# The first query chunk of two head blocks handled together in the self-attention of a hybrid decoder step

## The chip, the cores and the metric

The kernel runs on one core of one Trainium2 chip. The metric is device time in microseconds (us) for one launch, which computes the whole step. Three runs of the kernel before gave 1402.44, 1402.56 and 1403.07 us; the median is 1402.56 us. The profiled execution is one more run, of 1402.98 us, and its trace spans 1401.2 us from the first to the last instruction.

The engines are TensorE (PE in the profile, with its weight loads shown as PEld), VectorE (DVE), ScalarE (ACT), GpSimd (POOL) and SyncE (SP), which here only issues DMA. Each engine works through its own instructions in the order in which they stand in the program.

## The reference, cut to what matters

The step is one decoder layer for two groups of requests: a prompt of 256 tokens, and 8 single tokens with caches. The layer has a sliding-window self-attention and a state-space part (SSD) behind one input projection, then one output projection, then a cross-attention into 256 memory rows, then a feed-forward part with a short convolution. All of it is in fp32.

The change touches the self-attention of the prompt alone. The 256 positions are two chunks of 128, and the window is 128, so that a query sees its own chunk up to itself and the chunk before. For the first chunk there is no chunk before, and the queries see 128 keys at most; for the second chunk there are 256.

```python
def swa_banded(q, k, v, sinks):
    ...
    logits = jnp.einsum('bnqkgd,bnskd->bnkgqs', qb, kk, ...) * HEAD_DIM ** -0.5
    ...
    mask = ((diff >= 0) & (diff <= WINDOW))[None] & ((blk > 0) | (sj >= WINDOW)[None])
    p = sink_softmax(logits, mask[None, :, None, None], sinks.reshape(1, 1, N_KV_HEADS, Q_PER_KV, 1, 1))
    o = jnp.einsum('bnkgqs,bnskd->bnqkgd', p.astype(v.dtype), vv)
```

`sink_softmax` is a softmax with one more logit per head, the sink, whose share is dropped. There are 16 query heads of 64 and 4 key heads.

## The kernel before, in words

**Projections.** All large products are projections of 264 tokens (256 of the prompt and 8 samples) against weights that come from memory. Each fp32 operand is split into a high and a low part (`weights`: ACT writes `whi` at L85, DVE writes `wlo` at L86), and each product is made of three matmuls: L100 (`whi` by the high activations), L101 (`whi` by the low ones) and L102 (`wlo` by the high ones). A weight part is 128 x 1024; four of each kind are held.

**Stages.** The input projection goes in pairs of 128 output rows (`in_pair`). The first pairs give the keys, the values and the queries; then come 24 convolved rows for the SSD and 16 gate rows `z`. The self-attention, the SSD of four groups in two chunks each (`ssd_prompt`) and the sample part (`ssd_sample`) run beside the later pairs. Then the output projection begins with the half that comes from the attention (`AT`, L93), and goes on with the half from the SSD.

**The attention of the prompt.** Queries lie in `qT`, eight blocks j of 128 partitions, each of two heads of 64. `attn` is the same tile: the result takes the place of the queries. `kbd` holds the keys block-diagonally, so that one matmul gives the logits of both heads of a block. `attn_prompt(j)` takes the chunks c = 0 and c = 1 in a loop. I call one pass of that loop a unit; there are 16. A unit is this chain:

1. PE L525: the logits, 128 queries by two heads of 128 (c = 0) or 256 keys (c = 1), into the one bank `s` of the accumulators.
2. DVE L528 adds the mask and moves the logits into `pe`; L531 takes the maximum; L533, L534 and L535 are three small operations on 128 x 2 that scale it, compare it with the sink and prepare the sink's logit.
3. ACT L538: one exponential per head, with the sum of the row as a second result; L536 the exponential of the sink.
4. DVE L540 and L541: sum and reciprocal; L543: one multiplication per head.
5. PE L278 (the helper `tr`): transposes of 128 x 128 into a bank `t`, two in a unit with c = 0 and four in one with c = 1.
6. ACT L550 copies them into `pt`.
7. PE L554: the products with the values. Each head's product is 64 output rows wide, and is put into the lower or the upper 64 partitions of a bank `t`: two matmuls for c = 0, four for c = 1. In the trace an fp32 matmul stands as two records, so these are 4 and 8 records, with the shape 128*64.
8. ACT L556 copies the result into `attn`.

There are two banks `t`, and a unit uses two, one for the transposes and one for the result.

**What sets the order.** Within the opening of the kernel the order is written out by hand. From the attention on it is not: a planner simulates the program on its own costs, and puts each engine's instructions in the order in which they come up there, by priority. It may put attention instructions between any two matmuls of a projection. Weight parts and the emptying of accumulators have a higher priority. `marks["attn"]` is the last copy L556; the exponentials of the SSD (L743) are told to be issued after it (L741).

Of the kernel before, what the change touches and what calls it, by code (L numbers as in the profile page):

```python
# [47 lines left out]
def hybrid_decoder_step_kernel(ctx: ExitStack, tc: tile.TileContext, I, O):  # L48
# [11 lines left out]
    def psum(tag):  # L60
        return ps.tile([128, 512], F32, tag=tag, name=tag, bufs=banks[tag])
# [35 lines left out]
    marks = {}  # L97
# [165 lines left out]
    def pc(name, i=0, n=1):  # L263
        o = _PC[name][0]
        return par[:, o + i:o + i + n]
# [10 lines left out]
    def tr(out, in_):  # L276
        k = in_.shape[0]
        return PE.transpose(out, in_, cst[0:k, C_ID:C_ID + k])  # L278
# [237 lines left out]
    nsink = mp.tile([128, 16], F32, name="nsink")  # L516
    V.tensor_scalar(out=nsink, in0=pc("sink_p", 0, 16), scalar1=-1.0, scalar2=None, op0=ALU.mult)

    def attn_prompt(j, rq, nrq):
        pp = j // 4  # L520
        for c in range(2):
            nk = 128 * (c + 1)
            p = psum("s")
            s3 = p[:, 0:2 * nk].rearrange("p (h k) -> p h k", h=2)
            PE.matmul(s3, qT[:, j, c * 128:c * 128 + 128], kbd[:, pp, :, 0:nk], start=True, stop=True)  # L525
            e = mp.tile([128, 2, 256], F32, tag="h0", name="pe", bufs=3)
            ev = e[:, :, 0:nk]
            V.tensor_tensor(out=ev, in0=s3, in1=maskb[:, 256 - nk:256].unsqueeze(1).broadcast_to([128, 2, nk]), op=ALU.add)  # L528
            st = mp.tile([128, 8], F32, tag="st", name="st", bufs=4)
            mx, den, es = st[:, 0:2], st[:, 2:4], st[:, 4:6]  # L530
            V.tensor_reduce(out=mx, in_=ev, op=ALU.max, axis=AX.X)  # L531

            V.tensor_tensor(out=mx, in0=mx, in1=nrq[:, c, :], op=ALU.mult)  # L533
            V.tensor_tensor(out=mx, in0=mx, in1=nsink[:, 2 * j:2 * j + 2], op=ALU.min)  # L534
            V.tensor_tensor(out=es, in0=mx, in1=pc("sink_p", 2 * j, 2), op=ALU.add)  # L535
            S.activation(out=es, in_=es, func=AF.Exp)  # L536
            for h in range(2):
                S.activation(out=e[:, h, 0:nk], in_=e[:, h, 0:nk], func=AF.Exp, scale=rq[:, c, h:h + 1], bias=mx[:, h:h + 1],  # L538
                             accum_out=den[:, h:h + 1])
            V.tensor_tensor(out=den, in0=den, in1=es, op=ALU.add)  # L540
            V.reciprocal(out=den, in_=den)  # L541
            for h in range(2):
                V.tensor_scalar(out=e[:, h, 0:nk], in0=e[:, h, 0:nk], scalar1=den[:, h:h + 1], scalar2=None, op0=ALU.mult)  # L543
            p = psum("t")
            nb = c + 1
            for h in range(2):
                for kb in range(nb):
                    tr(p[:, (h * nb + kb) * 128:(h * nb + kb) * 128 + 128], e[:, h, kb * 128:kb * 128 + 128])
            pt = mp.tile([128, 4, 128], F32, tag="bc", name="pt", bufs=2)
            S.copy(out=pt[:, 0:2 * nb, :], in_=p[:, 0:2 * nk].rearrange("p (a q) -> p a q", q=128))  # L550
            o = psum("t")
            for h in range(2):
                for kb in range(nb):
                    PE.matmul(o[64 * h:64 * h + 64, 0:128], vn[:, kb, pp, 64 * h:64 * h + 64], pt[:, h * nb + kb, :],  # L554
                              start=kb == 0, stop=kb == nb - 1)
            marks["attn"] = S.copy(out=attn[:, j, c * 128:c * 128 + 128], in_=o[:, 0:128])  # L556


    qsq = [T3(apool, 4, tag="R", name=f"qsq{i}", bufs=4) for i in range(2)]
# [34 lines left out]
    nrqs = mp.tile([128, 2, 4, 4], F32, name="nrqs")  # L594
    V.tensor_scalar(out=nrqs, in0=rqs, scalar1=-1.0, scalar2=None, op0=ALU.mult)
    for j in range(8):
        d = 2 * (j // 4)
        attn_prompt(j, rqs[:, :, j % 4, d:d + 2], nrqs[:, :, j % 4, d:d + 2])

    def attn_sample():  # L600

# [909 lines left out]
```

## Time and profile before

| What | Value |
|---|---|
| median of three runs | 1402.56 us |
| profiled run | 1402.98 us |
| span of its trace | 1401.2 us |
| PE busy | 1396.6 us, 11519 records |
| DVE busy | 1051.5 us |
| ACT busy | 763.8 us |
| POOL busy | 93.3 us |
| attention, from the first logits to the last copy of L556 | 90.3 to 178.4 us |
| granted PE clock | 1.000 |

Busy times are the union of an engine's records. The ends of matmul records are modelled and the records overlap, so a busy PE is better judged by the distance between starts: between two matmuls of a projection that follow one another it is 0.12 us. The chain of waits is the same trace followed back from the last instruction; there each piece stands with the time by which it moved the chain on, which for PE is that distance.

### The profile page before, as it was taken

What the parts mean: (1) busy time and instruction counts of PE and PEld (TensorE: products, weight loads), DVE (VectorE), ACT (ScalarE), POOL (GpSimd) and SP (SyncE); (2) the same over time, 40 slices, a digit from 0 to 9 for tenths busy, and PEclk for the clock granted to TensorE, in tenths of its full rate; (3) what the DMA queues carried; (4) which work ended last, traced back from release to release, by engine and by line L of the source; (5) the groups of instructions that cost most, each with busy time, mean ns of one, the idle gap of its engine ahead of it and who ended that gap; (6) DMA issues with size and microseconds to landing.
All of it is one profiled execution on the core that took longest, in us unless ns stands there. A gap on an engine that the chain in (4) does not pass through costs nothing.

```text
span 1401.2 us, 29011 instructions
## 1 busy us (share of the span) xinstructions
PE 1396.6 (100%) x11519; PEld 1366.6 (98%) x11519; DVE 1051.5 (75%) x1906; ACT 763.8 (55%) x1255; POOL 93.3 (7%) x282
## 2 busy tenths in 40 slices
PE   9999999999999999999999999999999999999999
PEld 9988899999999999899999999999999999999998
DVE  8869879999987784578777775777577757765654
ACT  7556765556545554566565553555355535543532
POOL 0000001211000000001110000001000000000000
PEclk9999999999999999999999999999999999999999
DMA  7954358777776567665577765676567666656664
GB/s 298 325 174 132 121 180 251 223 247 255 247 227 233 187 227 260 223 245 189 189 243 226 249 216 183 212 249 215 187 215 234 197 190 196 197 176 186 188 186 138
DMA packets 89479, 298.33 MB, mean 213 GB/s; under 512 B 12032, under 2 KB 17152, under 8 KB 88832
## 3 DMA queue, kind: packets, MB, share of 16 engines
q1 hardware_dynamic: 83696, 277.35, 60.8%
q0 software_dynamic: 5504, 18.88, 4.2%
q8 instruction: 90, 1.47, 0.4%
q14 instruction: 45, 0.37, 0.1%
q10 hardware_dynamic: 144, 0.26, 0.0%
HBM read 280.77 MB, written 16.23 MB: 212 GB/s over the span
## 4 chain that ended last, share of the span: by engine, by line
PE 100%; DVE 0%; issue 0%
PE mm L100 21%; PE mm L101 21%; PE mm L102 21%; PE t L100 10%; PE t L101 10%; PE t L102 10%; PE t L240 1%; PE s L525 1%; PE t L278 1%; PE y L759 1%; PE t L554 1%; PE y L775 0%; PE s L240 0%; PE mm L240 0%; PE x L278 0%; PE x L1071 0%
## 5 line engine op out<-in xcount | busy, mean ns | idle before, releaser
L85 ACT CAST whi<-wraw 128x1024 fp32r<-128x1024 f32 x440 | 460.1, 1048 | 528.0 <-PE mm L101 273.3
L86 DVE TENSOR_TENSOR wlo<-wraw,whi 128x1024 fp32r<-128x1024 f32 x440 | 541.0, 1231 | 220.0 <-ACT whi L85 216.2
L100 PE MATMUL mm<-x2h,whi 128*128 128x264 f32 x704 | 199.8, 284 | 0.0
L100 PE MATMUL t<-x2h,whi 128*128 128x264 f32 x704 | 199.8, 284 | 0.0
L102 PE MATMUL t<-x2h,wlo 128*128 128x264 f32 x704 | 199.7, 284 | 0.0
L101 PE MATMUL t<-x2l,whi 128*128 128x264 f32 x704 | 199.6, 284 | 0.0
L101 PE MATMUL mm<-x2l,whi 128*128 128x264 f32 x704 | 199.5, 284 | 0.0
L102 PE MATMUL mm<-x2h,wlo 128*128 128x264 f32 x704 | 199.3, 283 | 0.0
L101 PE MATMUL mm<-hl,whi 128*128 128x264 f32 x704 | 198.7, 283 | 0.0
L102 PE MATMUL mm<-hh,wlo 128*128 128x264 f32 x704 | 198.2, 283 | 0.0
L100 PE MATMUL mm<-hh,whi 128*128 128x264 f32 x704 | 197.2, 284 | 0.0
L100 PE MATMUL mm<-xh,whi 128*128 128x264 f32 x576 | 167.5, 293 | 0.0
L101 PE MATMUL mm<-xl,whi 128*128 128x264 f32 x576 | 164.2, 287 | 0.0
L102 PE MATMUL mm<-xh,wlo 128*128 128x264 f32 x576 | 162.7, 288 | 0.0
L101 PEld LDWEIGHTS t<-x2l,whi 128*128 128x128 f32 x704 | 132.5, 188 | 0.0
L101 PEld LDWEIGHTS mm<-x2l,whi 128*128 128x128 f32 x704 | 132.5, 188 | 0.0
L100 PEld LDWEIGHTS mm<-x2h,whi 128*128 128x128 f32 x704 | 132.5, 188 | 0.0
L101 PEld LDWEIGHTS mm<-hl,whi 128*128 128x128 f32 x704 | 132.4, 188 | 0.0
L100 PEld LDWEIGHTS t<-x2h,whi 128*128 128x128 f32 x704 | 132.4, 188 | 0.0
L102 PEld LDWEIGHTS t<-x2h,wlo 128*128 128x128 f32 x704 | 132.2, 188 | 0.0
L102 PEld LDWEIGHTS mm<-x2h,wlo 128*128 128x128 f32 x704 | 132.1, 188 | 0.0
L102 PEld LDWEIGHTS mm<-hh,wlo 128*128 128x128 f32 x704 | 132.0, 188 | 0.0
(481 smaller groups left out, 2947.6 us busy)
## 6 DMA issues: line engine op xcount, KB each, us to landing
wraw<-in_w_up_dram SPq DMA_DIRECT2D x176, 512.0 KB, 4.3
wraw<-in_w_in_dram SPq DMA_DIRECT2D x96, 512.0 KB, 4.8
wraw<-in_w_dn_dram SPq DMA_DIRECT2D x88, 512.0 KB, 4.3
wraw<-in_w_out_dram SPq DMA_DIRECT2D x48, 512.0 KB, 4.4
h<-in_h_dram POOLq DMA_DIRECT2D x32, 256.0 KB, 5.0
hn<-in_h_dram SPq DMA_DIRECT2D x16, 512.0 KB, 4.4
out_state_s_dram<-hn POOLq DMA_DIRECT2D x16, 512.0 KB, 4.1
e<-dram_la SPq DMA_DIRECT2D x16, 256.0 KB, 4.5
```

Source lines behind the costliest of these rows:

```text
L85: S.copy(out=hi, in_=x)
L86: V.tensor_tensor(out=lo, in0=x, in1=hi.bitcast(F32), op=ALU.subtract)
L100: PE.matmul(out, wh, xh, start=start, stop=False)
L101: PE.matmul(out, wh, xl, start=False, stop=False)
L102: return PE.matmul(out, wl, xh, start=False, stop=stop)
L240: PE.matmul(first[c][:, :T], pre[k // 2][i][:, k % 2, c * 128:(c + 1) * 128], A[k // 8][x][:, k % 8, :], start=k + i + x == 0, stop=k == K ...
L278: return PE.transpose(out, in_, cst[0:k, C_ID:C_ID + k])
L525: PE.matmul(s3, qT[:, j, c * 128:c * 128 + 128], kbd[:, pp, :, 0:nk], start=True, stop=True)
L554: PE.matmul(o[64 * h:64 * h + 64, 0:128], vn[:, kb, pp, 64 * h:64 * h + 64], pt[:, h * nb + kb, :], start=kb == 0, stop=kb == nb - 1)
L759: PE.matmul(y[o:o + 64, (h // 2) * 128:(h // 2) * 128 + 128], xdt[:, h, :], es[h // 4][:, h % 4, :], start=True, stop=True)
```

## The change

The first chunk (c = 0) leaves `attn_prompt`, which now takes c as an argument and is called with c = 1 alone. A new function `attn_first(j)` takes the first chunk of the two blocks j and j + 1 at once, for j = 0, 2, 4 and 6, ahead of the second chunk of block j. The two logit matmuls of the pair go into the two halves of the one bank `s`. Mask, maximum, the small operations, the sum, the reciprocal and the multiplication are each one operation over four heads; the multiplication is now an operation of two tensors with the reciprocal broadcast. The exponentials stay one per head. The four transposes go into one bank and are copied at once, the four value products stand in one run, and one copy moves the result of both blocks. The tile `st` of the small values grows from 8 to 12 columns.

```diff
-    def attn_prompt(j, rq, nrq):
+    def attn_prompt(j, rq, nrq, c):
+
         pp = j // 4
-        for c in range(2):
-            nk = 128 * (c + 1)
...
+        nk = 128 * (c + 1)
...
+    def attn_first(j):
+
+        pp = j // 4
+        d, js = 2 * pp, slice(j % 4, j % 4 + 2)
+        rq, nrq = rqs[:, 0, js, d:d + 2], nrqs[:, 0, js, d:d + 2]
+        p = psum("s")
+        for i in range(2):
+            PE.matmul(p[:, 256 * i:256 * i + 256].rearrange("p (h k) -> p h k", h=2), qT[:, j + i, 0:128], kbd[:, pp, :, 0:128], start=True, stop=True)
+
+        e = mp.tile([128, 4, 128], F32, tag="h0", name="pe", bufs=3)
+        V.tensor_tensor(out=e, in0=p.rearrange("p (a k) -> p a k", a=4), in1=maskb[:, 128:256].unsqueeze(1).broadcast_to([128, 4, 128]), op=ALU.add)
+        st = mp.tile([128, 12], F32, tag="st", name="st", bufs=4)
+        mx, den, es = st[:, 0:4], st[:, 4:8], st[:, 8:12]
+        V.tensor_reduce(out=mx, in_=e, op=ALU.max, axis=AX.X)
+
+        mx2 = mx.rearrange("p (i h) -> p i h", i=2)
+        V.tensor_tensor(out=mx2, in0=mx2, in1=nrq, op=ALU.mult)
+        V.tensor_tensor(out=mx, in0=mx, in1=nsink[:, 2 * j:2 * j + 4], op=ALU.min)
+        V.tensor_tensor(out=es, in0=mx, in1=pc("sink_p", 2 * j, 4), op=ALU.add)
+        S.activation(out=es, in_=es, func=AF.Exp)
+        for i in range(4):
+            S.activation(out=e[:, i, :], in_=e[:, i, :], func=AF.Exp, scale=rq[:, i // 2, i % 2:i % 2 + 1], bias=mx[:, i:i + 1],
+                         accum_out=den[:, i:i + 1])
+        V.tensor_tensor(out=den, in0=den, in1=es, op=ALU.add)
+        V.reciprocal(out=den, in_=den)
+        V.tensor_tensor(out=e, in0=e, in1=den.unsqueeze(2).broadcast_to([128, 4, 128]), op=ALU.mult)
+        p = psum("t")
+        for i in range(4):
+            tr(p[:, i * 128:i * 128 + 128], e[:, i, :])
+        pt = mp.tile([128, 4, 128], F32, tag="bc", name="pt", bufs=2)
+        S.copy(out=pt, in_=p.rearrange("p (a q) -> p a q", q=128))
+        o = psum("t")
+        for i in range(4):
+            h = i % 2
+            PE.matmul(o[64 * h:64 * h + 64, 128 * (i // 2):128 * (i // 2) + 128], vn[:, 0, pp, 64 * h:64 * h + 64], pt[:, i, :], start=True, stop=True)
+        S.copy(out=attn[:, j:j + 2, 0:128], in_=o[:, 0:256].rearrange("p (i q) -> p i q", i=2))
...
     for j in range(8):
+        if j % 2 == 0:
+            attn_first(j)
         d = 2 * (j // 4)
-        attn_prompt(j, rqs[:, :, j % 4, d:d + 2], nrqs[:, :, j % 4, d:d + 2])
+        attn_prompt(j, rqs[:, :, j % 4, d:d + 2], nrqs[:, :, j % 4, d:d + 2], 1)
```

More of the change, by code (lines that the diff above doesn't have):

```diff
@@ L517, in hybrid_decoder_step_kernel @@
     V.tensor_scalar(out=nsink, in0=pc("sink_p", 0, 16), scalar1=-1.0, scalar2=None, op0=ALU.mult)
-    def attn_prompt(j, rq, nrq):
+    def attn_prompt(j, rq, nrq, c):
         pp = j // 4
-        for c in range(2):
-            nk = 128 * (c + 1)
[L523 to L556, printed above, removed]
@@ new lines, in attn_prompt @@
+        nk = 128 * (c + 1)
+        p = psum("s")
+        s3 = p[:, 0:2 * nk].rearrange("p (h k) -> p h k", h=2)
+        PE.matmul(s3, qT[:, j, c * 128:c * 128 + 128], kbd[:, pp, :, 0:nk], start=True, stop=True)
+        e = mp.tile([128, 2, 256], F32, tag="h0", name="pe", bufs=3)
+        ev = e[:, :, 0:nk]
+        V.tensor_tensor(out=ev, in0=s3, in1=maskb[:, 256 - nk:256].unsqueeze(1).broadcast_to([128, 2, nk]), op=ALU.add)
+        st = mp.tile([128, 12], F32, tag="st", name="st", bufs=4)
@@ new lines, in attn_prompt @@
+        mx, den, es = st[:, 0:2], st[:, 2:4], st[:, 4:6]
+        V.tensor_reduce(out=mx, in_=ev, op=ALU.max, axis=AX.X)
+        V.tensor_tensor(out=mx, in0=mx, in1=nrq[:, c, :], op=ALU.mult)
+        V.tensor_tensor(out=mx, in0=mx, in1=nsink[:, 2 * j:2 * j + 2], op=ALU.min)
+        V.tensor_tensor(out=es, in0=mx, in1=pc("sink_p", 2 * j, 2), op=ALU.add)
+        S.activation(out=es, in_=es, func=AF.Exp)
+        for h in range(2):
+            S.activation(out=e[:, h, 0:nk], in_=e[:, h, 0:nk], func=AF.Exp, scale=rq[:, c, h:h + 1], bias=mx[:, h:h + 1],
+                         accum_out=den[:, h:h + 1])
@@ new lines, in attn_prompt @@
+        V.tensor_tensor(out=den, in0=den, in1=es, op=ALU.add)
+        V.reciprocal(out=den, in_=den)
+        for h in range(2):
+            V.tensor_scalar(out=e[:, h, 0:nk], in0=e[:, h, 0:nk], scalar1=den[:, h:h + 1], scalar2=None, op0=ALU.mult)
+        p = psum("t")
+        nb = c + 1
+        for h in range(2):
+            for kb in range(nb):
+                tr(p[:, (h * nb + kb) * 128:(h * nb + kb) * 128 + 128], e[:, h, kb * 128:kb * 128 + 128])
+        pt = mp.tile([128, 4, 128], F32, tag="bc", name="pt", bufs=2)
```

14 lines of the change are left out of this document (added).

## The prediction, as put on record before the changed kernel ran

> **What bounds the kernel now.** I read the page first: the busy times, and the chain of work that ended last.
>
> ```profile
> span 1401.2 us, 29011 instructions
> ...
> PE 1396.6 (100%) x11519; PEld 1366.6 (98%) x11519; DVE 1051.5 (75%) x1906; ACT 763.8 (55%) x1255; POOL 93.3 (7%) x282
> ...
> PE 100%; DVE 0%; issue 0%
> ```
>
> The chain is PE from end to end. A PE that is busy by modelled ends could still wait, so the second view is the list of who waited for whom, for PE alone. It has one row:
>
> ```profile
> PE x L201 <- DVE eps L274: 1.2, 1, 1.2
> ```
>
> That is the start of the kernel. After it PE waits for nobody, so the time is the sum of what PE's own instructions take, and only a change of that sum, or a new wait of PE, moves the end. The third view is the chain of waits piece by piece, which gives the step of each run of matmuls. Its columns are start, microseconds, what.
>
> ```profile
> 97.96 0.43 PE s L525 x2
> 101.75 0.86 PE s L525 x2
> 104.68 0.37 PE t L554 x4
> 105.05 0.32 PE mm L101
> 105.60 0.12 PE mm L101
> 107.51 0.22 PE t L278 x2
> 111.24 0.59 PE t L554 x8
> 111.83 0.32 PE mm L101
> ...
> 129.37 0.44 PE t L278 x4
> 132.97 0.59 PE t L554 x8
> 133.56 0.37 PE t L278 x2
> ...
> 361.79 1.02 PE y L759 x16
> 362.81 0.32 PE t L102
> ```
>
> An ordinary projection matmul moves the chain by 0.12 us. A run of value products (L554) costs 0.37 us with 4 records and 0.59 with 8, so 0.055 a record and 0.37 - 4 x 0.055 = 0.15 fixed. The instruction behind it pays too: the projection matmul takes 0.32 in place of 0.12, and two transposes take 0.37 in place of 0.22. One visit to this 64-wide shape thus has a fixed price of 0.15 + 0.20 = 0.35 us where a projection follows and 0.15 + 0.15 = 0.30 where transposes follow, beside its records. The SSD's products (L759, the same shape, 16 records) bear it out: 0.15 + 16 x 0.055 = 1.03 against 1.02, and again 0.32 behind.
>
> **The change on PE.** No matmul is added or removed: 16 logit matmuls, 48 transposes and 48 value products stay.
>
> - Value products. Eight runs of 4 records become four of 8. Records cost the same; four visits go. That is 4 x 0.30 = 1.2 to 4 x 0.35 = 1.4 us less. I take 1.3. The other end of this term is nothing, if the planner cuts the new runs apart (a rival below).
> - Logits. Two separate runs of 0.43 become one of four records. The run with twice the columns takes 0.86 = 2 x 0.43, so there is no fixed price to save: 0.
> - Transposes. Two runs of two, 0.22 each, become one of four; the trace has 0.44 for that: 0. If a pair stands directly behind a value run, it carries the switch, which the first item counts.
>
> Sum on PE: -1.3 us.
>
> **The change beside PE.** The multiplication by a broadcast reciprocal over 512 columns does not stand in the trace; the nearest rows are the SSD's L745 and L754, of the same width and kind.
>
> ```profile
> L528 DVE TENSOR_TENSOR pe<-s,cst 128x512 f32<-128x512 f32 x8 | 5.5, 689 | 2.4 <-PE s L525 1.4 <-PE t L278 0.9
> L531 DVE TENSOR_REDUCE st<-pe 128x2 f32<-128x512 f32 x8 | 5.4, 678 | 0.0
> L543 DVE TENSOR_SCALAR pe<-pe,st 128x128 f32<-128x128 f32 x16 | 3.8, 282 | 0.0
> L528 DVE TENSOR_TENSOR pe<-s,cst 128x256 f32<-128x256 f32 x8 | 3.4, 422 | 3.6 <-PE s L525 3.4
> L531 DVE TENSOR_REDUCE st<-pe 128x2 f32<-128x256 f32 x8 | 3.3, 414 | 0.0
> L533 DVE TENSOR_TENSOR st<-st,nrqs 128x2 f32<-128x2 f32 x16 | 2.5, 155 | 0.0
> ...
> L745 DVE TENSOR_TENSOR e<-e,s 128x512 f32<-128x512 f32 x16 | 10.5, 679 | 0.0
> L754 DVE TENSOR_TENSOR xw<-x,de 128x512 f32<-128x512 f32 x8 | 5.4, 679 | 0.0
> ```
>
> Before, two units with c = 0 cost DVE 2 x (422 + 414 + 5 x 155 + 2 x 282) = 4350 ns, taking all five small operations at L533's price. After, one pair costs 689 + 678 + 5 x 155 + 680 = 2820. DVE loses 1.5 us a pair, 6.1 us in all. ACT loses some copies and sink exponentials. Neither is on the chain, so I cost both at nothing; the cover is PE's queue of projection matmuls, which never ran dry. If the cover were gone, this would be a gain and not a loss.
>
> **Waits that it adds.** The pair's unit is longer: four exponentials in a row before its transposes may go. On PE the transposes and value products stand in order with projection matmuls behind them, so a late one would hold up the projection. The planner places them where its simulation has them ready, and in the trace PE did not wait for any of the 32 such groups; I take 0, and the upper end is a rival's price. Another wait would come if the planner took the copy into `attn[:, j:j+2, 0:128]` for a write of everything between its ends: the second chunk's queries lie there, and would wait for the whole first unit.
>
> ```profile
> L550 ACT COPY pt<-t x16: 350/472/592, 101.4 to 174.4; 128x256 f32<-128x256 f32 x8, 128x512 f32<-128x512 f32 x8
> ...
> L556 ACT COPY attn<-t x16: 246/266/268, 105.4 to 178.1; 128x128 f32<-128x128 f32 x16
> ...
> L604 ACT ACTIVATE qs_sq<-attn x1: 240/240/240, 83.3 to 83.3; 128x64 f32<-128x64 f32 x1
> ...
> 178.14 0.27 ACT L556 COPY attn<-t 128x128 f32<-128x128 f32 x1 [1.86 <-PE t L554]
> 178.30 1.28 ACT L743 ACTIVATE e<-e,la 128x128 f32<-128x128 f32 x4
> ```
>
> The first three rows have the shortest, middle and longest duration in ns, then the first and last start; the last two are single instructions. L604 reads columns 256 to 263 of all blocks of that tile, stands behind all attention in the program, and ran at 83.3 us, before the first write at 105.4. Columns are told apart, so I cost this at nothing.
>
> **What moves.** The 16 units were paced at (174.4 - 101.4) / 15 = 4.9 us. Twelve units at that pace are 11 x 4.9 = 54 us, so the last copy should come near 160 us rather than 178; an estimate. The SSD's L743 begins right behind that copy and so begins earlier too. The work that is late next is DVE's, in the SSD; the first row below is a window's busy time of PE, PEld, DVE, ACT and POOL, the others are single instructions with start and duration:
>
> ```profile
> 240.00:290.00 50.00, 50.00 (x419) 48.42 (x418) 50.00 (x99) 29.39 (x54) 11.21 (x12) 1.00 0.77 246
> ...
> 271.27 1.21 DVE L86 TENSOR_TENSOR wlo<-wraw,whi 128x1024 fp32r<-128x1024 f32 x1
> ...
> 273.30 0.28 PE L102 MATMUL mm<-xh,wlo 128*128 128x264 f32 x1
> ```
>
> From 240 to 290 us DVE is busy all 50.00 us, like PE, and the low weight part that is done at 272.48 is first used at 273.30: 0.8 us of cover. An earlier start of the SSD and 6.1 us less DVE work should widen this.
>
> **The sum.** The profiled run took 1402.98 us, a span of 1401.2 and 1.8 around it. Less 1.3 it gives 1401.7. That run lies 0.4 above the median of 1402.56, so against the median the forecast is 1401.3 us. The planner lays all matmuls after the attention anew; with 12 value runs that may each meet the 0.30 or the 0.35 neighbour (12 x 0.05 = 0.6) and one 64-wide run cut or joined elsewhere (0.35), its own range is 1 us to each side, 1400.3 to 1402.3.
>
> **The rivals.**
>
> *No merge.* The planner cuts 64-wide runs where its simulation has other work ready. It did so with one group of eight SSD products, 16 records elsewhere:
>
> ```profile
> 373.63 0.66 PE L759 MATMUL y<-e,xdt 128*64 128x128 f32 x8
> ...
> 380.60 0.66 PE L759 MATMUL y<-e,xdt 128*64 128x128 f32 x8
> ```
>
> If it cuts all four new runs, or pays as much elsewhere, the time stays: 1402.6. Against it: all 16 value runs before were whole, since their products become ready together through one copy. Chance 0.12.
>
> *The weights come late: slower.* With 0.8 us of cover in the stage in which DVE is full, a new order decides. If one SSD chunk's four wide operations (two L745, L754 and its twin L751, 4 x 0.68 = 2.7 us) come ahead of a low weight part that has least cover, PE waits 2.7 - 0.8 = 1.9 us. Three such parts make 5.7 - 1.3 = +4.4: 1407.0. The point from which it decides is more than 0.8 us of added DVE work ahead of such a part. For it speaks the full DVE; against it the 6.1 us taken off DVE and the earlier start. Chance 0.10.
>
> *DVE sets the pace there: faster.* If the full DVE, not PE, had set the pace, the 6.1 us would come off too: 1402.56 - 1.3 - 6.1 = 1395.2. Against it: PE's list of waits has no row there. Chance 0.04.
>
> *The two halves overlap: a little faster.* In the new run the heads alternate between the lower and the upper 64 rows at each product; before, in units with c = 1, two products of one half followed each other. If alternate halves ran at the same time, each run of 8 would lose half its streaming, 4 x 0.055 = 0.22 us, four times 0.9: 1401.3 - 0.9 = 1400.4. The Trainium skill has a rule for this, in "TensorEngine Tiling (Array Packing)", under "Key Properties": different tiles can load weights and multiply in parallel. The trace does not bear it out here: L759 alternates its halves at every product and still pays 0.055 a record. Chance 0.04.
>
> **How the numbers follow.** The forecast has 0.70. A measurement of this kernel can tell about 0.2% from no change, 2.8 us, so faster is below 1399.8 and slower above 1405.4. Faster: 0.04 of the DVE rival, 0.03 from the forecast's lower tail and 0.01 of the overlap, 0.08. Slower: 0.10 of the late weights and 0.02 for a first chunk's unit that holds up PE, 0.12. The same: 0.80. The range goes from 1399.6, which takes in the overlap, to 1403.8, which takes in the rival without a merge and one wait of about 1.2 us; late weights and the DVE rival are left out.
>
> **What would show it.** After the change the chain of waits should show twelve runs of value products, all of 8 records and near 0.59 us, each with one dearer instruction behind it, and so four visits fewer; PE's list of waits should stay at one row; DVE should be busy about 6 us less; the last copy into `attn` should come near 160 us. A second row in PE's waits, most of all one for `wlo`, would make the prediction wrong on the slow side; a fall of more than 2.8 us with PE's list unchanged would say that the chain had a price that I did not read.

## The result: 0.28% slower, and the profile after

The changed kernel took 1406.89 us in the median of seven runs (1405.39 to 1409.66), the kernel before 1403.11 in seven (1402.44 to 1404.07). The ratio is 1.0028, with a 95% interval of 1.0018 to 1.0038: slower by 0.28%, and even the lower end of the interval, 0.18%, lies close to the 0.2% that a measurement can tell. Forecast were 1401.3 us, within 1399.6 to 1403.8, and "the same". The time lies where the rival of the late weights had put it, at 1407.0.

The page of the changed kernel first: span, busy times, shares of the chain.

```profile
span 1404.8 us, 28946 instructions
...
PE 1396.2 (99%) x11519; PEld 1366.3 (97%) x11519; DVE 1050.0 (75%) x1866; ACT 764.3 (54%) x1243; POOL 90.9 (6%) x282
...
PE 97%; DVE 1%; DMA 1%; ACT 0%; issue 0%; SPq 0%; DVEq 0%; ACTq 0%
```

PE is busy 0.4 us less than before (1396.6), though the span is 3.6 longer. The chain, 100% PE before, now leaves PE for DVE and a DMA. PE's list of waits, which had one row, has four:

```profile
PE mm L102 <- DVE wlo L86: 2.3, 3, 1.0
PE x L201 <- DVE eps L274: 1.2, 1, 1.2
PE t L240 <- ACT whi L183: 1.1, 1, 1.1
PE y L798 <- ACT hp L816: 0.4, 1, 0.4
```

The second row was there before. The third belongs to the opening, which is the same in both kernels, and comes and goes between executions (0 to 1.2 us in the profiles below, of both kernels). The first and the last are new. Measured by the distance between the starts of PE's matmuls, they make 3.4 us in four places: 0.6 at 198.9 us, 1.1 at 208.9, 1.2 at 211.6 for `wlo`, and 0.5 at 229 for the SSD's state.

The value products did what was forecast. From the chain of waits, the runs of the merged first chunk (L592) and of the second chunk (L554):

```profile
107.96 0.59 PE t L592 x8
115.39 0.59 PE t L554 x8
...
158.74 0.59 PE t L592 x8
163.53 0.60 PE t L554 x8
170.09 0.59 PE t L554 x8
```

Twelve runs, all of 8 records. The last copies into `attn`, though, came at 170.7 us and not near 160 (the rows give the shortest, middle and longest duration in ns, then the first and last start):

```profile
L556 ACT COPY attn<-t x8: 257/265/265, 116.0 to 170.7; 128x128 f32<-128x128 f32 x8
L593 ACT COPY attn<-t x4: 349/351/372, 109.8 to 159.8; 128x256 f32<-128x256 f32 x4
```

Now the place of the waits. These are DVE's instructions between 198 and 213 us: start, duration, what, and in brackets its idle time and who ended it.

```profile
198.27 1.22 DVE L86 TENSOR_TENSOR wlo<-wraw,whi 128x1024 fp32r<-128x1024 f32 x1
199.41 0.68 DVE L842 TENSOR_TENSOR h<-h,cb 128x512 f32<-128x512 f32 x1
...
201.50 1.22 DVE L86 TENSOR_TENSOR wlo<-wraw,whi 128x1024 fp32r<-128x1024 f32 x1
202.64 0.68 DVE L843 TENSOR_REDUCE ych<-h 128x4 f32<-128x512 f32 x1
...
205.07 1.30 DVE L842 TENSOR_TENSOR h<-h,cb 128x512 f32<-128x512 f32 x2 [0.62 <-DMA cb<-dram_bc]
206.28 0.48 DVE L718 SCALAR_TENSOR_TENSOR c<-u,par,c 128x256 f32<-128x256 f32 x1
206.68 1.28 DVE L784 TENSOR_TENSOR e<-e,s 128x512 f32<-128x512 f32 x2
207.87 0.48 DVE L718 SCALAR_TENSOR_TENSOR c<-u,par,c 128x256 f32<-128x256 f32 x1
208.27 0.68 DVE L843 TENSOR_REDUCE ych<-h 128x4 f32<-128x512 f32 x1
208.86 1.22 DVE L86 TENSOR_TENSOR wlo<-wraw,whi 128x1024 fp32r<-128x1024 f32 x1
```

And PE's first use of the part that is done at 208.86 + 1.22 = 210.08, with the next one:

```profile
208.92 0.28 PE L101 MATMUL mm<-xl,whi 128*128 128x264 f32 x1
210.14 0.39 PE L102 MATMUL mm<-xh,wlo 128*128 128x264 f32 x1 [0.93 <-DVE wlo L86]
...
211.58 0.28 PE L101 MATMUL mm<-xl,whi 128*128 128x264 f32 x1
212.86 0.39 PE L102 MATMUL mm<-xh,wlo 128*128 128x264 f32 x1 [1.00 <-DVE wlo L86]
```

A weight part feeds 24 matmuls of 0.12 us, so PE takes a new low part about every 2.9 us. Between the parts at 201.50 and 208.86 DVE lets 7.4 us go by, with the sample's products and sums (L842, L843), the SSD's products (L784), the convolution (L718) and 0.6 us of waiting for a load in between. The sample work (`ssd_sample`) is the part that moved: its first sum begins at 188.86 us, before it was 199.52.

Just ahead of it comes a block on ACT that both kernels have. Right behind the last copy of the attention ACT does the SSD's exponentials and their neighbours:

```profile
170.74 0.27 ACT L556 COPY attn<-t 128x128 f32<-128x128 f32 x1 [0.62 <-PE t L554]
170.90 1.28 ACT L782 ACTIVATE e<-e,la 128x128 f32<-128x128 f32 x4
172.20 1.28 ACT L282 ACT_TABLE_LOAD   x1
...
173.71 2.44 ACT L782 ACTIVATE e<-e,la 128x128 f32<-128x128 f32 x8
176.17 1.28 ACT L783 ACT_TABLE_LOAD   x1
...
178.00 1.03 ACT L85 CAST whi<-wraw 128x1024 fp32r<-128x1024 f32 x1
```

For 7 us no weight is cast. I call the time from the end of a low part to the start of the first matmul that reads it the cover. It was 8.8 us ahead of this block in both kernels, and falls to 1.4 in the changed kernel and to 2.4 in the one before. But it recovers before the sample work begins: to 6.2 us in the changed kernel, and in the one before to 6.7 (a part ends at 195.90 and is first read at 202.60). The difference comes behind that. Before, the next parts have 5.9, 5.0, 2.6, 4.2 and 4.7 us of cover. After, they have 2.2, 0.8 and 0.06. These are rows of DVE, with the sample's first two products, and the first reads of the two parts by PE:

```profile
185.52 1.22 DVE L86 TENSOR_TENSOR wlo<-wraw,whi 128x1024 fp32r<-128x1024 f32 x1
...
187.36 0.68 DVE L842 TENSOR_TENSOR h<-h,cb 128x512 f32<-128x512 f32 x1
...
191.04 0.69 DVE L842 TENSOR_TENSOR h<-h,cb 128x512 f32<-128x512 f32 x1 [1.51 <-DMA h<-in_h_dram]
...
192.45 1.22 DVE L86 TENSOR_TENSOR wlo<-wraw,whi 128x1024 fp32r<-128x1024 f32 x1
```

```profile
192.99 0.28 PE L102 MATMUL mm<-xh,wlo 128*128 128x264 f32 x1
...
195.91 0.28 PE L102 MATMUL mm<-xh,wlo 128*128 128x264 f32 x1
```

Between the end of the one part, 186.74, and the start of the next, 192.45, DVE lets 5.7 us go by, 1.5 of them in waiting for a load, and the cover falls from 192.99 - 186.74 = 6.2 us to 195.91 - 193.67 = 2.2.

So far this is a reading of two traces: PE saved some 1.0 us and lost 3.4, and the waits lie where the sample work now stands on DVE. Whether that work is the cause, or the load that it waits for, or the block on ACT ahead of it, or the merged runs themselves, is a matter for runs.

### The profile page after: what moved, and what is told of

Read it like the earlier page. It is cut to its first block, busy times and chain, and to the rows that moved or that the text cites. A ratio compares the mean times of both kernels' runs of the same rounds, so it can differ in the third digit from the quotient of the medians.

```text
span 1404.8 us, 28946 instructions
## 1 busy us (share of the span) xinstructions
PE 1396.2 (99%) x11519; PEld 1366.3 (97%) x11519; DVE 1050.0 (75%) x1866; ACT 764.3 (54%) x1243; POOL 90.9 (6%) x282
## 4 chain that ended last, share of the span: by engine, by line
PE 97%; DVE 1%; DMA 1%; ACT 0%; issue 0%; SPq 0%; DVEq 0%; ACTq 0%
PE mm L100 21%; PE mm L101 21%; PE mm L102 20%; PE t L100 10%; PE t L101 10%; PE t L102 10%; PE t L240 1%; PE t L278 1%; PE y L798 1%; PE s L525 1%; PE y L814 0%; DMA open<-in_open_dram 0%; PE s L240 0%; PE mm L240 0%; PE t L554 0%; PE x L1110 0%
## 5 line engine op out<-in xcount | busy, mean ns | idle before, releaser
L100 PE MATMUL mm<-x2h,whi 128*128 128x264 f32 x704 | 199.9, 284 | 0.0
L100 PE MATMUL t<-x2h,whi 128*128 128x264 f32 x704 | 199.8, 284 | 0.0
L102 PE MATMUL t<-x2h,wlo 128*128 128x264 f32 x704 | 199.7, 284 | 0.0
L101 PE MATMUL mm<-x2l,whi 128*128 128x264 f32 x704 | 199.6, 284 | 0.0
L101 PE MATMUL t<-x2l,whi 128*128 128x264 f32 x704 | 199.5, 283 | 0.0
L100 PE MATMUL mm<-hh,whi 128*128 128x264 f32 x704 | 197.2, 284 | 0.0
L100 PE MATMUL mm<-xh,whi 128*128 128x264 f32 x576 | 166.6, 292 | 0.0
L100 PEld LDWEIGHTS mm<-x2h,whi 128*128 128x128 f32 x704 | 132.5, 188 | 0.1
L100 PEld LDWEIGHTS t<-x2h,whi 128*128 128x128 f32 x704 | 132.4, 188 | 0.0
```

The lines of the kernel that those rows point to most:

```text
L100: PE.matmul(out, wh, xh, start=start, stop=False)
L101: PE.matmul(out, wh, xl, start=False, stop=False)
L102: return PE.matmul(out, wl, xh, start=False, stop=stop)
```

## The experiments

"Before" in each comparison are runs of the kernel before on the same chip; their medians lie between 1403.19 and 1403.36. All medians and intervals stand in the table at the end of this section.

### Is it the load? e1, e2, e3 and e4

DVE waits 0.6 us for the load of `cb`. e1 takes away half of these loads, using the factors of the first half of a group for both halves (which changes the sample's output); e2 moves the sample's first group behind the next convolution in the program; e3 and e4 undo one half of the merge each.

```diff
 e1, in ssd_sample:
-            cb = mp.tile([128, 4, 128], F32, tag="cb", name="cb", bufs=1)
-            nc.gpsimd.dma_start(out=cb, in_=dram_bc[1][8 * g + 4 * q:8 * g + 4 * q + 4, :].partition_broadcast(128))
+            if q == 0:
+                cb = mp.tile([128, 4, 128], F32, tag="cb", name="cb", bufs=1)
+                nc.gpsimd.dma_start(out=cb, in_=dram_bc[1][8 * g:8 * g + 4, :].partition_broadcast(128))
 e2:
-    ssd_sample(0)
     ssd_prompt(1)
     conv_group(3)
+    ssd_sample(0)
 e3, in attn_first, behind the common softmax:
+        for k in range(2):
+            p = psum("t")
+            for h in range(2):
+                tr(p[:, h * 128:h * 128 + 128], e[:, 2 * k + h, :])
...
+            S.copy(out=attn[:, j + k, 0:128], in_=o[:, 0:128])
 e4: the reverse; mask to multiplication once per block as before, then
 the four transposes, their copy, the four value products and the result's copy as after
```

> The changed kernel with the row of C for the SSD's samples (cb) loaded once per group in place of twice; the second four samples are then multiplied with the first four samples' C, so that part of the SSD's sample output is left out. Theory A (the planner has moved the sample work forward; DVE waits in order for the second load of cb, which can only start when the first is used up, and the low weight part behind it comes late): PE's waits for wlo near 200 to 212 us, 2.9 us in sum, fall to under 0.5, and the time to about 1402 to 1403. Theory B (DVE simply has too much to do there, whatever the load): the waits stay above 2 us and the time above 1405. Theory C (the merged run itself costs PE): the time stays near 1407 and the steps of the value runs are dearer than 0.59 us.

> The changed kernel with the first group of sample work (ssd_sample(0)) put behind the last convolutions in the program, so that the planner has no reason to begin it near 187 us. Theory A and theory B: no wait of PE for wlo before 215 us, and unless the work collides later the time is 1402 to 1403. Theory C: no gain, about 1407.

> The changed kernel with its common softmax, but transposes, copy, value products and result copy for each block by itself, as before: 16 value runs again, 8 of 4 records and 8 of 8. If the four merged runs save what the prediction says, PE's own work is about 1.3 us more than in the changed kernel. Theory A and B: what decides is whether PE waits for wlo in this plan; with none the time is 1402.5 to 1403.5, with as many as in the changed kernel about 1408. Theory C: about 1403 whatever the waits.

> The changed kernel with the softmax of each block by itself, and the transposes, copy, value products and result copy of two blocks together: 12 value runs. PE's own work as in the changed kernel, 1.3 us less than before. Theory A and B: the time is 1401.5 to 1402.5 if PE does not wait for wlo in this plan, and longer by exactly its waits if it does. Theory C: about 1407 with no wait to explain it.

e1 took 1409.78 us, 2.9 more than the changed kernel, and kept its waits for `wlo`, two of them, 2.1 us, though the second load of `cb` was gone; another row for 2.4 us came at 305 us:

```profile
PE t L100 <- DVE u L864: 2.4, 1, 2.4
PE mm L102 <- DVE wlo L86: 2.1, 2, 1.1
```

The load of `cb` is not the cause. e2 was 1407.04: DVE and PE got the same order as without the edit, so the place in the program is not what sets when the planner takes the sample work. (Its tiles share their three buffers, `tag="h0"`, with the attention's `pe`, which may be what ties it to the attention's end; no run changes that.) e2 is thus the changed kernel once more and tells nothing apart: its waits for `wlo` are nearly the same, 2.8 us against 2.9, while the wait of 0.5 us for the SSD's state came at 325 us and not at 229. e3 comes out like the kernel before, 1403.25, with the attention's end at 177.8 us and no wait in the stage; and e4, with the value products merged but the softmax apart, has its attention's end at 178.3 and 1405.29 us. So neither half alone shortens the attention, only both do. e4 has no wait at 200 us either, but it loses its gain later: 1.1 us at 369 us for the SSD's state (the row of L800), and 1.6 at the join where the output projection turns to the SSD's half, at 420 us:

```profile
PE mm L101 <- DVE yl L93: 0.7, 1, 0.7
PE y L800 <- ACT hp L818: 0.7, 1, 0.7
PE mm L100 <- ACT yh L93: 0.4, 1, 0.4
```

The kernel before has little to spare at that join. This row of DVE holds the two low parts of the SSD's result for the samples. The first ends at 419.87 us, and PE reads it at 420.79; the second ends at 420.00 and is not read before 426.59:

```profile
419.65 0.35 DVE L93 TENSOR_TENSOR yl<-ysam,yh 128x64 fp32r<-128x64 f32 x2
```

A kernel that saves PE time arrives there earlier, and 0.9 us is all that it can be earlier unless `gate_sample`, the closing steps of the sample, ends earlier too.

### Is it the sample work on DVE? e5 to e8

e5 keeps group 0's operations but feeds them a constant tile, so that they wait for no load (this changes the sample's output); e8 is the same edit on the kernel before. e7 leaves group 0's sample work out (its output is zero there). e6 keeps all the work and holds the first four products of group 0 back until the accumulators of the convolved row marked `u5` are emptied, at about 196 us.

```diff
 e5 and e8:
-                V.tensor_tensor(out=h0, in0=h0, in1=cb, op=ALU.mult)
+                if g: (load and product as before)
+                else:
+                    c4 = cst[:, 0:512].rearrange("p (a n) -> p a n", a=4)
+                    V.tensor_tensor(out=h0, in0=c4, in1=c4, op=ALU.mult)
 e7:
+            if g == 0:
+                V.memset(ych[:, 0:4, rows], 0.0)
+                continue
 e6:
+                if g == 0 and q == 0:
+                    with tc.issue_after(marks["u5"].ins):
+                        V.tensor_tensor(out=h0, in0=h0, in1=cb, op=ALU.mult)
```

> The changed kernel with the first group's eight sample multiplications and reductions done on a constant tile that is already there, in place of states and C rows loaded for them: the same DVE operations, no load to wait for. The SSD's sample output of the first group is thereby not the reference's. Theory A (DVE waits in order for a load, with weight parts behind): no wait of PE above 0.5 us from 185 to 230 us and a time of 1401.5 to 1403. Theory B (the DVE work itself is too much there): PE waits for wlo 2 us or more near 200 to 212 us all the same, and the time is above 1405.

> The control for the run on resident data: the kernel before with the same edit (the first group's sample multiplications on a constant tile, its output left out of the comparison). The kernel before had no wait of PE there to lose, so theories A and B expect no change, 1402.5 to 1403.5; a gain of 1 us or more would say that the edit itself saves time and that the run on the changed kernel proves nothing.

> The changed kernel with the first four sample multiplications of the first group told to be issued behind the accumulator of row block 5 (near 200 us), which is where the kernel before has them. Theory A: their loads have landed by then, DVE waits for no load before 215 us, PE's waits for wlo go, 1401.5 to 1403. Theory B: the work is only moved; waits of 2 us or more come back somewhere from 200 to 300 us, and the time is above 1404.

> The changed kernel without the first group's sample multiplications, reductions and loads at all (their result is set to zero): 11 us of DVE work less between 187 and 240 us. Theories A and B: no wait of PE for wlo from 185 to 240 us; the time is 1401.5 to 1402.5, which is what the merged value runs are worth when nothing else binds. Theory C (the merged run costs PE): above 1404 all the same.

e5 still waits 2.1 us for one `wlo` at 209.7 us, and took 1406.56. That ends the load as a cause: the operations are enough. e7 missed its purpose: the planner put group 1's sample work into the free place, at 188.7 us, and the waits stayed (1406.75). e6 is the clean one. With the same work, only later, all waits at 198 to 212 us are gone. But it took 1405.24, because the closing steps now come late for the join. They end at 422.97 us; in the changed kernel they end at 407.21, nearly 17 us ahead of their use, so this join has no part in that kernel's loss:

```profile
PE y L295 <- DVE accy L895: 1.7, 1, 1.7
...
PE mm L101 <- DVE yl L93: 0.5, 1, 0.5
```

e8, on the kernel before, has no wait in the stage. It is 1.3 us slower than before because the planner cut its SSD products into three more runs (28 visits to the 64-wide shape in place of 25).

### Without the sample's products: e9, e10, e13, e14

If the sample's work on DVE is the trouble, the merge should show its gain where that work is not there. e9 and e10 leave out the loads, products and sums of all groups, in the kernel after and before.

```diff
 e9, e10, in ssd_sample:
+            V.memset(ych[:, 4 * g:4 * g + 4, rows], 0.0)     (in place of loads, products and sums)
 e13, e14: the same, and in gate_sample
-        V.tensor_tensor(out=ych, in0=ych, in1=dsb[:, :, 8:16], op=ALU.mult)
+        V.tensor_tensor(out=ych, in0=zsam, in1=dsb[:, :, 8:16], op=ALU.mult)
```

> The changed kernel without any of the sample multiplications, reductions and their loads (all four groups; the result is set to zero, so the SSD's sample output is left out): 43 us of DVE work less in the SSD stage. Theory D, formed after the first eight runs (from about 185 to 420 us DVE and PE are both full, so PE work that is saved ahead of that stage comes back as PE waiting for DVE: for low weight parts where DVE takes the sample work early, for the sample's tail at 420 us where it takes it late): PE waits for nothing from 90 to 420 us, and the time is 1401 to 1402. Theory C (the merge itself costs PE): above 1404.

> The kernel before with the same left out. Theory D: PE waited for nothing before either, so 1402.5 to 1403.5, and the changed kernel without samples is 1.0 to 1.5 us faster than this one: the worth of the four saved value runs where DVE does not bind. Theory C: this one is the faster of the two.

> The changed kernel without the sample's state products (no loads of the state and of the factors for them, no products and sums; the sample's output is taken from another tile instead, at the place where it is used late). This repeats e9 without the early operation that delayed the attention in both e9 and e10. With some 4 fewer visits to the narrow shape than its control and no weight wait behind the attention, theory A (the merge saves PE time by visits, and its loss is the waiting that it brings) gives 1.0 to 1.5 us less than e14, about 1401.3 us, with fewer than 1 us of waits on PE in the stage. Theory B (the merge itself costs time on PE, whatever DVE does) gives e14 or more.

> Control of e13: the kernel before without the sample's state products, in the same way. Theory A: about 1402.6 us, between -1.0 and +0.5 us of the kernel before, with 24 or 25 visits to the narrow shape. Theory B: the same time or less than e13.

In e9 and e10 the first of the closing steps had nothing left to wait for but a load, so it went ahead of the attention on DVE and held up the queries for some 2 us in both (row "PE mm L100 <- DVE attn L408", 1.7 and 2.1 us): 1404.26 against 1405.58. e13 and e14 take its operand from the late tile `zsam` in place of `ych`, and there it no longer goes ahead: 1402.01 against 1403.77. With DVE relieved, the merged kernel is the faster one in both pairs. From the queries' norms to the join the profiled runs of e13 and e14 differ by 334.5 - 332.1 = 2.4 us: 1.2 is one wait for the SSD's state in e14, and 1.2 goes with the visits, 20 against 24. In the opening e13 is 1.4 us later than e14, 0.8 of it by a wait for the queries at 72 us that stands in no other profile. Read as a saving by the merge alone, the medians give 0.6 to 1.8, without and with e14's wait.

e13 also tells what the block on ACT does by itself. The cover falls to 1.4 us there too (a part ends at 183.52 and is read at 184.88), but without the sample's products no part from there to 298 us has less than 4.2 us, and PE waits for none.

### Relief by another engine: e11 and e12

Here the small copies into `cnew` and `zsam`, 40 in all, go from DVE to POOL, in the kernel after and before.

```diff
-            V.tensor_copy(out=cnew[:, bi, :], in_=u[:, TP:])
+            P.tensor_copy(out=cnew[:, bi, :], in_=u[:, TP:])
...
-            V.tensor_copy(out=zsam[:, 2 * i + m, :], in_=z[:, TP:])
+            P.tensor_copy(out=zsam[:, 2 * i + m, :], in_=z[:, TP:])
```

> The changed kernel, whole, with the 24 copies into cnew and the 16 into zsam (0.16 us each on DVE, 6.6 us in the stage) done by POOL. Theory D: DVE has 6.6 us less to do in the full stage, PE's waits shrink from 3.5 us to under 1, and the time is 1401.5 to 1403.5, faster than the changed kernel by 3 us or more. If DVE's load is not what binds, the time stays near 1406.9.

> The control: the kernel before with the same copies on POOL. Theory D: no wait of PE to remove, 1402.5 to 1403.5, and any difference is the planner's new order. If POOL's copies hold up the projection, slower.

e11 was the slowest of all, 1411.13 us. Its attention ended at 167.7 us, earlier still, and its waits grew:

```profile
PE mm L100 <- ACT whi L85: 2.1, 1, 2.1
PE mm L102 <- DVE wlo L86: 1.8, 4, 0.6
PE y L798 <- ACT hp L816: 1.5, 1, 1.5
...
```

That the attention's end moved by another 3 us and the waits doubled fits the theory, but POOL also issues the sample's loads, so this run changes more than one thing, and why its later waits came is left open. e12 was 1.6 us slower than the kernel before.

### Order alone: e15 to e18

e15 takes e6 and gives `gate_sample` high priority; e16 does the latter to the kernel before. e17 puts the closing steps of e15 into another order, so that what does not need the last state product comes first; e18 gives the last group's sample work high priority as well.

```diff
 e15, e16:
+            with tc.high_priority():
+                gate_sample()
 e17, in gate_sample:
+        V.tensor_tensor(out=t..., in0=xds..., in1=cbs..., op=ALU.mult)
+        V.tensor_tensor(out=ysam, in0=ysam, in1=t, op=ALU.add)
+        S.activation(out=t, in_=zsam, func=AF.Tanh, scale=0.5)
+        V.scalar_tensor_tensor(out=zsam, in0=t, scalar=1.0, in1=zsam, op0=ALU.add, op1=ALU.mult)
         V.tensor_tensor(out=ych, in0=ych, in1=dsb[:, :, 8:16], op=ALU.mult)
         V.tensor_tensor(out=ysam, in0=ysam, in1=ych, op=ALU.add)
         V.tensor_tensor(out=ysam, in0=ysam, in1=zsam, op=ALU.mult)
...
 e18: e17, and
+            with tc.high_priority():
+                ssd_sample(3)
```

> The changed kernel with two edits in the order of DVE's work alone: group 0's first sample products are held back until about 200 us, as in e6, and the sample's closing steps, which end just ahead of the join at 420 us, are given high priority. Theory A (the loss is work of DVE that lands where PE's cover is thin): no weight wait at 198 to 212 us, none at the join, and 1401.5 to 1402.5 us, which would be 1 to 2 us less than the kernel before. Rival (the plan has no slack anywhere between 185 and 420 us, and what is taken from one join is given back at another): the waits of 2 us or so appear elsewhere in that stage and the time stays at 1404 to 1406 us.

> Control of e15: the kernel before with the sample's closing steps at high priority. It has 0.78 us to spare at the join, so theory A and the rival both expect no change, 1402.5 to 1403.5 us; a time over 1404 us would say that the priority moves other work of DVE into the way.

> e15 with the sample's closing steps in another order, so that what does not need the last state product (the second product and its sum, the tanh and its factor) comes first and five serial steps instead of eight stand between the last state product and the split that the output projection waits for. In e15 the nine steps came about 2.5 us apart, behind one weight part each, and ended at 422.25 us, 1.2 us after the first use of their high part. Theory A (the loss is DVE work that lands where PE's cover is thin): the closing steps end some 5 us earlier, the two waits of 0.8 and 0.7 us at the join are gone, and the time is 1402.0 to 1403.0 us. The rival (the plan gives back elsewhere what is taken from one join): 1404 to 1406 us, with waits of 1.5 us or more in another place of the stage.

> e17 with the last group's sample work at high priority too, so that its products come earlier on DVE. Theory A: no wait at the join, 1402.0 to 1403.0 us, unless the earlier sample work thins the weights' cover somewhere between 360 and 400 us, which would show as a row for wlo. The rival: 1404 to 1406 us.

e15 was a miss: 1405.01 us. The priority did not help, since the closing steps wait for one another and each stands behind a weight part; PE waited 0.8 and 0.7 us at the join. e16 changed nothing (1403.25). e17 ends the closing steps at 418.59 us and not at 422.25, and its list of waits is that of the kernel before:

```profile
PE x L201 <- DVE eps L274: 1.2, 1, 1.2
```

Its span, from its page, is 1.4 us shorter than that of the kernel before:

```profile
span 1399.8 us, 28945 instructions
```

It took 1402.24 us, e18 1402.91. e17 is 4.65 us below the changed kernel, with the same work on every engine, and no run of the one reached a run of the other (1401.61 to 1403.30 against 1405.39 to 1409.66). Against the kernel before it is 1.0 us faster by the medians, ratio 0.9994 with 0.9985 to 1.0002, so that gain is about the size that was forecast but lies within what a measurement can tell. The new order of the closing steps was not run in the kernel before; since PE does not wait at that join there, it should gain nothing, but that is argued.

How little DVE's busy time tells about this shows in one window, 200 to 215 us. The row has the busy time of PE, PEld, DVE, ACT and POOL. First the changed kernel, then e17:

```profile
200.00:215.00 15.00, 13.07 (x106) 12.63 (x105) 14.31 (x31) 6.30 (x8) 2.15 (x4) 1.00 0.64 205
```

```profile
200.00:215.00 15.00, 15.00 (x127) 15.00 (x126) 15.00 (x28) 6.96 (x8) 2.44 (x5) 1.00 0.80 260
```

In e17 DVE is the busier one, and PE loses nothing; its low parts there are done 4.5 to 6.4 us ahead of their use.

### All runs

"End" is the end of the last copy of the attention into `attn`, "sum" the start of the sample's first sum, "visits" the runs of the 64-wide shape (L554, L592, L759 or L798), "waits" PE's waits between the attention and the join, by distances between starts.

| kernel | median us (runs) | ratio [95%] | end | sum | visits | waits, where |
|---|---|---|---|---|---|---|
| before | 1403.11 (7) | 1 | 178.4 | 199.5 | 25 | none |
| after | 1406.89 (7) | 1.0028 [1.0018, 1.0038] | 171.0 | 188.9 | 22 | 2.9 at 199 to 213, 0.5 at 229 |
| e1 | 1409.78 (5) | 1.0045 [1.0032, 1.0057] | 170.6 | 188.5 | 22 | 2.5 at 199 to 212, 3.0 at 305 |
| e2 | 1407.04 (6) | 1.0029 [1.0018, 1.0041] | 170.7 | 188.5 | 22 | 2.8 at 199 to 212, 0.5 at 325 |
| e3 | 1403.25 (11) | 1.0000 [0.9991, 1.0009] | 177.8 | 199.3 | 25 | none |
| e4 | 1405.29 (11) | 1.0014 [1.0005, 1.0023] | 178.3 | 197.9 | 21 | 1.1 at 369, 1.6 at 420 |
| e5 | 1406.56 (10) | 1.0024 [1.0014, 1.0034] | 170.7 | 186.8 | 21 | 2.1 at 210, 1.7 at 305 and 325 |
| e6 | 1405.24 (10) | 1.0016 [1.0006, 1.0026] | 171.0 | 199.7 | 21 | 2.5 at 419 to 422 |
| e7 | 1406.75 (10) | 1.0026 [1.0016, 1.0035] | 170.8 | 188.7 | 22 | 3.4 at 199 to 213, 0.9 at 229 |
| e8 (before) | 1404.54 (10) | 1.0009 [1.0000, 1.0019] | 179.0 | 197.3 | 28 | none |
| e9 | 1404.26 (11) | 1.0006 [0.9997, 1.0015] | 173.2 | - | 20 | 0.7 at 335 |
| e10 (before) | 1405.58 (11) | 1.0021 [1.0012, 1.0029] | 180.8 | - | 24 | none |
| e11 | 1411.13 (5) | 1.0057 [1.0044, 1.0069] | 167.7 | 187.0 | 23 | 8.0 in many places |
| e12 (before) | 1404.86 (11) | 1.0013 [1.0005, 1.0022] | 180.4 | 203.3 | 26 | 0.8 at 205, 1.2 at 281 |
| e13 | 1402.01 (11) | 0.9992 [0.9983, 1.0001] | 171.7 | - | 20 | none |
| e14 (before) | 1403.77 (11) | 1.0007 [0.9998, 1.0015] | 178.2 | - | 24 | 1.2 at 255 |
| e15 | 1405.01 (11) | 1.0013 [1.0004, 1.0022] | 171.0 | 199.8 | 21 | 1.8 at 419 to 422 |
| e16 (before) | 1403.25 (11) | 1.0001 [0.9992, 1.0010] | 178.5 | 199.6 | 25 | none |
| e17 | 1402.24 (11) | 0.9994 [0.9985, 1.0002] | 170.4 | 198.8 | 21 | none |
| e18 | 1402.91 (11) | 0.9998 [0.9989, 1.0007] | 170.7 | 199.3 | 22 | none |

The split is without exception: each kernel whose first sum begins at 187 to 189 us waits for `wlo` at 199 to 213, and none does whose first sum begins at 197 or later.

One sum holds the table together. From the last matmul of the queries' norms (86 to 88 us) to the first product of the SSD's half at the join (419 to 424 us), the time is 325.3 us + 0.34 a visit + the waits in it, to within 0.4 us for 18 of the 20 kernels; e1 and e11, with the most waits, took 1.7 and 1.4 us more than it gives. Both constants are fitted to these runs. Before: 325.3 + 25 x 0.34 = 333.8, measured 333.7. After: 325.3 + 22 x 0.34 + 3.4 = 336.2, measured 336.5. e17: 325.3 + 21 x 0.34 = 332.4, measured 332.5.

## Why the prediction was wrong, point by point

- *PE's sum: four visits less, -1.3 us.* The price was right. It held as 0.34 us a visit, against 0.30 to 0.35 forecast; e17 against the kernel before, neither with a wait, gives 333.7 - 332.5 = 1.2 us for four visits. The Trainium skill says in "TensorEngine Tiling (Array Packing)", under "Key Properties", that a change of tiling mode drains TensorE; the trace agrees, and 0.34 us is what one way in and out cost here. The count was off by one in the changed kernel: the planner cut one more SSD group, so three visits went and not four, about -1.0 us. The forecast's range had room for that.
- *Logits and transposes: 0.* Right: four logit records took 0.86 to 0.87 us as forecast, and nothing is left for these in the sum above.
- *DVE loses 6.1 us, costed at nothing.* By the groups of its attention rows DVE lost 5.2 us (38.7 before, 33.5 after); on the page, where overlapping instructions count once, 1.5. It brought nothing, as forecast.
- *The columns of `attn` are told apart.* Right; no unit waits for the pair's copy.
- *"The last copy should come near 160 us."* It came at 170.7. The step took the pace of a unit as fixed at 4.9 us; twelve longer units went at (170.09 - 107.96) / 11 = 5.6 us between their value runs, from a later start. This error of 10 us did not hurt by its size; 7.4 us earlier was enough.
- *"I take 0" for the waits, and "an earlier start of the SSD and 6.1 us less DVE work should widen" the cover: this is the step that failed, and with the wrong sign.* The step read one place, 272 us, where cover was 0.8 us, and there it was right: in the changed kernel a part ends at 272.70 and is read at 276.92, 4.2 us of cover. But it took an earlier start as more time for everything, and what starts earlier is DVE's optional work. The sample work begins 10.7 us earlier, takes the weights' cover from 6.2 us to nothing within three parts, and brings 2.9 us of waits for `wlo`; with 0.5 for the SSD's state PE waits 3.4 us in place of 0. e5, e6 and e13 show it: no load is needed for the waits, the same work 10 us later leaves none there, and without it the cover stays. Why these operations use up more cover at 187 us than at 197 is not shown. One of the first waits 1.5 us for a load, but e5 loses its cover without such a wait.
- *"The planner places them where its simulation has them ready, and in the trace PE did not wait for any of the 32 such groups".* This held for the attention itself. It was carried over to the rest of the plan, where a change of 10 us in one part's readiness sets the order anew. A second thin place, 0.9 us at the join at 420 us, was not looked for; e6 and e15 gave the gain back there, and e4 a part of it.
- *The rival of the late weights, 1407.0, chance 0.10.* It had the right mechanism, DVE work ahead of a low part with little cover, and nearly the right time. Its place and work were others: at 199 to 213 us and not 240 to 290, by the sample work and not the SSD's four wide operations, and 2.9 us in three waits and not three times 1.9. That its time lies 0.1 us from the measured one is luck, because the rest came from elsewhere: one visit less saved, 0.5 us for the state, and 0.8 us of opening and tail by which the profiled executions differ.
- *The other rivals.* No merge: refuted by the chain of waits. DVE as the pace: refuted, since relief of DVE in e13 and e14 brought no such fall. Overlap of the halves: no run of 8 was below 0.59 us.
- *What would show it* named a row for `wlo` in PE's waits as the sign of being wrong on the slow side. That is the row that came.

Of the 3.8 us between the medians the profiled executions show 3.6 in the span: -1.0 by visits and +3.4 by waits give 2.4 of 2.7 us in the stage, and 0.8 lies in the opening and behind the join, where the instructions are the same. That the changed kernel also spreads more from run to run (4.3 us against 1.6) was not explained.

## What to carry to other kernels

An engine that waits for nothing is the bound, but it says nothing about how near the next wait is: read, at every place where one engine feeds it, how long ahead of its use each part is done, and look for the thinnest places, here 0.9 us at a join. Ask too what other work of the feeding engine may come in between: here 6.2 us were used up within three weight parts. Where a planner orders work by readiness, ending one stage earlier moves the optional work behind it too, and a saving of 1 us is less than what one such move can cost. Then the saving has to be shipped with the order that keeps it: hold the optional work back, and shorten the chain ahead of the join that is reached earlier.

## What the runs showed of the hardware that was not expected

A copy of 128 x 8 elements took 0.15 to 0.17 us on DVE in the changed kernel, and on POOL in e11 between 0.19 and 2.46 us, with a middle of 1.12. First the changed kernel's row, then e11's:

```profile
L864 DVE COPY zsam<-u x16: 151/158/166, 292.7 to 384.4; 128x8 f32<-128x8 f32 x16
```

```profile
L864 POOL COPY zsam<-u x16: 189/1116/2457, 284.4 to 382.9; 128x8 f32<-128x8 f32 x16
```

The Trainium skill has a rule that fits, in "SBUF — State Buffer", under "Summary: rules for kernel authors": while VectorE runs an operation with two inputs from SBUF, a GpSimd operation that reads SBUF is blocked until it ends. The traces of e11 and e12 agree with it. Of their 80 copies 43 took more than 0.3 us, and each of these 43 ends 0.05 to 0.09 us behind the end of a DVE operation with two operands in SBUF, which is where the tiles lie that are not accumulators. One such copy ends at 310.21 + 1.11 = 311.32 us, and the low part beside it at 310.06 + 1.21 = 311.27:

```profile
310.21 1.11 POOL L864 COPY zsam<-u 128x8 f32<-128x8 f32 x1 [4.07 <-DVE u L863]
```

```profile
310.06 1.21 DVE L86 TENSOR_TENSOR wlo<-wraw,whi 128x1024 fp32r<-128x1024 f32 x1
```

The other 37 took 185 to 255 ns, and many of them ran beside DVE's reductions or its operations with one operand in the accumulators. No run takes DVE's part in it away, but 43 ends of 43 leave little room for another cause. Whether this is also why e11 was slow is not shown.

The price of a visit to the 64-wide shape was steady to a degree that was not expected: one figure of 0.34 us accounts for kernels with 20 to 28 visits, from 332.1 us for the stage with 20 visits (e13) to 334.9 with 28 (e8), neither with a wait: 2.73 / 8 = 0.34.
